# Reading the moving operand of 73 channel blocks, of the opening and of the 256-column products two rows at a time

## The chip, the cores and the metric

The kernel runs on one core of a Trainium2 chip. The time is device microseconds of one execution. The core has a matrix engine (TensorE, PE in the profile; its weight loads are listed as PEld), three engines for elementwise work (VectorE or DVE, ScalarE or ACT, GpSimd or POOL) and SyncE (SP), which issues most transfers.

## The reference

One layer of an encoder on 256 tokens of 2048 channels, in float32:

```python
proj = h @ w_in                       # 2048 x 16416: q, k, v, r, gates, hy_u, gate_logits
y_gla = _gla_branch(q, k, v, r, ...)  # gated linear attention, both directions
y_hy = _hyena_branch(hy_u, ...)       # short convolution, then two long ones by Fourier transforms
merged = g0 * (y_gla @ w_gla_o) + g1 * (y_hy @ w_hy_o)
h = _layernorm(ALPHA * h + merged @ w_out, ln1_g, ln1_b)
ff = jnp.square(jax.nn.relu(h @ w_ff1)) @ w_ff2      # 2048 -> 8192 -> 2048
h = _layernorm(ALPHA * h + ff, ln2_g, ln2_b)
```

## The kernel before

**High and low parts.** Every large product is made in three: each operand is split into a rounded part (ScalarE casts it, L104 or L1242) and what is left (VectorE subtracts, L105 or L1239), and high x high, high x low and low x high are added in PSUM. An activation such as `xT` or `hT` lies as [128, 16 k-tiles, 2 parts, 256 tokens]. In each k-tile the 256 tokens lie with the 128 even ones first and the 128 odd ones after them (for `xT`), or the first 128 and then the other 128 of the kernel's own order (for `hT`).

**Two kinds of blocks.** A weight block of 1 MB is used in one of two ways.

In a *token block* (`token_half`, L244 to L255) the activation is stationary and the weights move past it, 512 columns at a time. The weights lie in memory with even columns first, and the matmul reads them with `in_turn`: word 0 of the first row of 256, word 0 of the second, word 1 of the first, and so on. So the result has its columns in natural order. The products of the second MLP weight in the paired loop (`form_products`, L1375 to L1383) read in the same way.

In a *channel block* (`channel_products`, L187 to L200) the weights are stationary and the activation moves. For each of 16 k-tiles there is one matmul of 512 columns (the weight's high part against both parts of the activation, L193) and one of 256 (the weight's low part against the activation's high part, L197). Both read the activation straight on. The result has the token order of the activation, so `channel_sum` (L208 to L213) adds the two halves of a PSUM bank and writes q and k with every second word skipped (`in_order`, `by_parity`), which puts tokens in natural order. Channel blocks compute q and k (12 blocks, `channel_pair`) and the first MLP product f (64 blocks).

**The opening** (L336 to L342) is a product of channel kind that starts while the input still arrives: five blocks at once (the gates' low-rank part and four blocks of q), piece by piece.

**The output projection and the last product** use 256 columns of weights at a time in their last parts (`column_half`, L1072 to L1083); these weights lie in natural order and are read straight on. So are those of one 512-column part of the last product (`fourth`, L1553, which gives `token_half` the reading `lambda w: w`).

**The MLP.** `ff1_first` (L1343) makes the first 8 blocks of f. Three of them are begun with the first 128 tokens while the second 128 are still being normalised (`begin_three`, `finish_block`); the others go through `channel_products`. Then comes the paired loop `ff_pairs` (L1421) with 56 slots. A slot has 21 products of the second weight (3 + 2 groups before, 2 after) around one channel block of f. Its order is pinned by program order on all engines. In a slot VectorE splits the slot's weights (six subtractions), adds two pairs of weight units, adds f's two halves (`quad_sum`, L1247 to L1253, f's halves straight on) and, in 27 of the slots from slot 5 on, the *forms*: combinations of f that the second product needs (`forms`, L1261), which are made by VectorE, rounded by ScalarE and subtracted by VectorE again. At the ends of the seven runs of slots it also adds the seven PSUM sums of the second product into SBUF.

**Buffers around it.** Of the four PSUM buffers of the main pool three are held by the second product during the loop, so f has one: the next block of f starts when `quad_sum` has read the one before. Split weights have three buffers in turn for each part.

Of the kernel before, what the change touches and what calls it, by code (L numbers as in the profile page):

```python
# [13 lines left out]
ALU = mybir.AluOpType  # L14
DRAM = bass.MemoryType.DRAM

P = 128
D = 2048
L = 256
NT = L // P  # L20
# [11 lines left out]
LEAD = 8  # L32
# [17 lines left out]
def block_kernel(  # L50
# [128 lines left out]
        fetch()  # L179
        return queue.popleft()  # L180

    FULL = slice(0, L)

    def channel_psum(name):
        return psum_main(name).rearrange("p (a b) -> p a b", a=2)

    def channel_products(ps, act, half, kts, ts=FULL, opens=True):  # L187
        hi, lo = half
        at = [(kt, slice(kt % 8 * P, (kt % 8 + 1) * P)) for kt in kts]

        def high():
            for kt, js in at:
                MM(ps[:, :, ts], hi[:, js], act[:, kt, :, ts], start=(kt == 0 and opens), stop=(kt == KT - 1))  # L193

        def low():
            for kt, js in at:
                MM(ps[:, 0, ts], lo[:, js], act[:, kt, 0, ts], start=False, stop=False)  # L197

        for part in (high, low) if kts[0] == 0 else (low, high):
            part()  # L200

    def by_parity(ap):
        return ap.rearrange("p (t m) -> p t m", t=NT)

    def in_order(ap):
        return ap.rearrange("p (m t) -> p t m", t=NT)

    def channel_sum(dst, ps, name, scale=1.0):  # L208
        low = base.tile([P, L], F32, tag="low", name=name)
        with tc.high_priority():  # L210
            nc.scalar.activation(low, ps[:, 1], AF.Copy, scale=scale)
            nc.vector.scalar_tensor_tensor(in_order(dst), by_parity(ps[:, 0]), scale, by_parity(low),
                                           op0=ALU.mult, op1=ALU.add)  # L213

    def channel_pair(act, name, dst, scale=1.0):
        for c in range(2):
# [16 lines left out]
    def finish_block(ps, act, parts, n):  # L233
        for h in range(n):
            high_by_tokens(ps, act, parts[h], range(8 * h, 8 * h + 8), slice(P, L))
        for h in range(n):
            low_of_all(ps, act, parts[h], range(8 * h, 8 * h + 8))
        for h in range(n, 2):
            channel_products(ps, act, parts[h], range(8 * h, 8 * h + 8))

    def in_turn(w):
        return w.rearrange("p (a b) -> p b a", a=2)

    def token_half(pss, act, half, tbs, kt0, ends=(0, KT - 1), order=lambda ins: ins, moving=in_turn):  # L244
        hi, lo = half
# [54 lines left out]
    with tc.tile_pool(name="xp", bufs=1) as xp, tc.tile_pool(name="xq", bufs=1) as xq:  # L300
        def units(pool, tag, n, **kw):
            t = pool.tile([P, n, OPENING * P], F32R, tag=tag, name=f"open_{tag}", **kw)
            return lambda a, b: t[:, a:b].rearrange("p k (b j) -> p k b j", b=OPENING)

        pieces = {}
        for k0, n in PIECES[::-1]:
            if k0 < 10:
                pieces[k0] = xp.tile([P, n, KROW], F32, tag=f"xw{k0}", name=f"xw{k0}")
            else:
                raw = wp.tile([P, D], F32, tag="raw", bufs=3, name=f"xw{k0}")  # L310
                pieces[k0] = raw[:, 0:n * KROW].rearrange("p (k c) -> p k c", k=n)
        wu = xp.tile([P, 512], F32, tag="wu", name="wu")
        nc.vector.memset(wu, 0.0)
        pw = psum_side("warm")
        for _ in range(2):
            MM(pw, wu[:, 0:P], wu, start=True, stop=True)

        fetched[0] = OPENING
        for k0, n in PIECES:
            nc.sync.dma_start(pieces[k0], first[k0 * P:(k0 + n) * P, :].rearrange("(p k) c -> p k c", k=n))  # L320

        u_y, u_g, u_k, u_q, u_x = (units(base, "yT", 12), units(qp, "G", 6), units(qp, "k", 3), units(qp, "q", 2),
                                   units(xq, "sp", 3))
        places = {6: (u_y(6, 8), u_y(8, 10)), 8: (u_y(10, 12), u_g(0, 2)), 10: (u_g(2, 4), u_g(4, 6)),
                  12: (u_k(0, 2), u_q(0, 2))}
        for i in range(3):
            t = weight_half(-1, i, True)
            places[i] = [v[:, 0:OPENING * P].rearrange("p (k b j) -> p k b j", k=1, b=OPENING) for v in t]
            places[3 + i] = (u_y(2 * i, 2 * i + 1), u_y(2 * i + 1, 2 * i + 2))
        places[14], places[15] = (u_k(2, 3), u_x(0, 1)), (u_x(1, 2), u_x(2, 3))  # L330

        def part_of(kt, part):
            k0 = kt if kt in places else kt - 1
            return places[k0][part][:, kt - k0]

        def products(kts, b, part):  # L336
            for kt in kts:
                w = part_of(kt, part)[:, b]
                if part == 0:
                    MM(open_ps[b], w, xT[:, kt], start=(kt == 0), stop=(b == 0 and kt == KT - 1))  # L340
                elif b:
                    MM(open_ps[b][:, 0], w, xT[:, kt, 0], start=False, stop=(kt == KT - 1))  # L342

        turned = False
        for k0, n in PIECES:
            raw = pieces[k0]
            kts = range(k0, k0 + n)
            split_hi_lo(xT[:, k0:k0 + n, 0], xT[:, k0:k0 + n, 1], raw[:, :, 0:L])
            w = raw[:, :, L:].rearrange("p k (b j) -> p k b j", b=OPENING)

            def split(hi, lo, w, first=0):
                nc.scalar.copy(hi, w)
                if first == 0:
                    low = hi[:, :, 0, 96:]
                    nc.vector.tensor_tensor(low, w[:, :, 0, 96:], low.bitcast(F32), op=ALU.subtract)
                bs = slice(1 - first, None)
                nc.vector.tensor_tensor(lo[:, :, bs], w[:, :, bs], hi[:, :, bs].bitcast(F32), op=ALU.subtract)

            if k0 == 0:
                hi, lo = places[0]  # L360
                for bs in (slice(0, 3), slice(3, OPENING)):
                    split(hi[:, :, bs], lo[:, :, bs], w[:, :, bs], bs.start and 1)
            elif k0 == 14:
                for i in range(n):
                    split(places[k0 + i][0], places[k0 + i][1], w[:, i:i + 1])
            else:
                split(places[k0][0], places[k0][1], w)
            if k0 + n == KT:
                for b in range(OPENING):
                    for part in (0, 1):  # L370
                        products(kts, b, part)
            else:
                for part in (1, 0) if turned else (0, 1):
                    for b in range(OPENING):
                        products(kts, b, part)
                turned = not turned and k0 >= 6 and k0 < 12
# [152 lines left out]

    pa = open_ps[0]  # L530
    nc.scalar.copy(a_low, pa[:, 1])
    nc.vector.tensor_tensor(in_order(a_sum[:, 0]), by_parity(pa[:, 0]), by_parity(a_low), op=ALU.add)
    nc.scalar.copy(as_sb, a_sum[:, 0])
    nc.vector.tensor_tensor(as_sb[64:96, :], a_sum[64:96, 0], as_sb[64:96, :].bitcast(F32), op=ALU.subtract)
    pump()
# [536 lines left out]
    def column_half(pss, act, half, ch, tbs, kt0, ends=(0, KT - 1), order=lambda ins: ins):  # L1072
        hi, lo = half
        for j in range(2):
            kt = kt0 + j
            cs = slice(j * 512 + ch * 256, j * 512 + ch * 256 + 256)
            for tb in tbs:
                ps = pss[tb][ch][:, 0:256]
                sh = act[:, kt, 0, tb * P:(tb + 1) * P]
                sl = act[:, kt, 1, tb * P:(tb + 1) * P]  # L1080
                order(MM(ps, sh, hi[:, cs], start=(kt == ends[0]), stop=False))
                order(MM(ps, sh, lo[:, cs], start=False, stop=False))
                order(MM(ps, sl, hi[:, cs], start=False, stop=(kt == ends[1])))  # L1083

    def column_products(pss, act, blocks, tbs, b0):
        for ch in range(2):
# [157 lines left out]
    def rest(lo, src, hi):  # L1244
        return VT(lo, src, hi.bitcast(F32), ALU.subtract)

    def quad_sum(i, c, ps, name):  # L1247
        low = base.tile([P, L], F32, tag="low", name=name)
        dst = quads(i)[:, 2 * c:2 * c + 2][:, ::-1]
        halves = [a.rearrange("p (t j) -> p t j", j=P) for a in (ps[:, 0], low)]  # L1250
        with tc.high_priority():
            cast(low, ps[:, 1])
            return VT(dst, halves[0], halves[1], ALU.add)  # L1253
# [89 lines left out]
    def ff1_first():  # L1343
        begun = begin_three()
        for c2 in range(LEAD // 2):
            for c in range(2):
                if begun:
                    ps, parts, n = begun.pop(0)
                    finish_block(ps, hT, parts, n)
                else:  # L1350
                    ps = channel_psum(f"f{c2}_{c}")
                    parts = next_block()
                    for h in range(2):
                        channel_products(ps, hT, parts[h], range(8 * h, 8 * h + 8))
                summed = quad_sum(c2, c, ps, f"f{c2}_l{c}")
                at = 2 * c2 + c
                if at in (LEAD - 4, LEAD - 3):
                    block_load(at - LEAD + 4)
# [191 lines left out]
    add_ff(left[0], 0, 1024, 512, order=keep)  # L1550
    keep(split_hi_lo(zg[0], zg[1], z1[:, 1, 0:1024])[1])
    for half, kt in fourth:
        token_half([ps], f3, half, [0], kt, ENDS, keep, lambda w: w)  # L1553
    pss = [psum_main(f"w2_33_1{ch}") for ch in range(2)]
    add_ff(ps, 0, 1536, 512)
    rs, nb = norm_scale(st2, 0, "2")
# [54 lines left out]
def _layout(a):  # L1611
# [5 lines left out]
        k, n = w.shape  # L1617
        return w.reshape(k // P, P, n // P, P).transpose(2, 1, 0, 3).reshape(n // P, P, -1)

    def even_first(w):  # L1620
        return w.reshape(-1, 256, 2).transpose(0, 2, 1).reshape(w.shape)

    def tok(w):
        k, n = w.shape
# [14 lines left out]
    for i in range(NCH // 2):  # L1639
# [13 lines left out]
    wblk = np.concatenate(  # L1653
        [chan(ga), chan(seg["q"]), chan(seg["k"])]
        + [even_first(w) for w in [tok(seg["r"]), tok(seg["v"]), g1] + ubl + [g2, tok(a["w_hy_o"][0]), wo[:-4]]]
        + [wo[-4:], f1[:LEAD], pairs, even_first(rest[:-2]), rest[-2:]], axis=0)

    first = np.concatenate(
        [a["x"][0].T.reshape(KT, P, P, NT).transpose(1, 0, 3, 2).reshape(P, KT, L)] + [w.reshape(P, KT, P) for w in wblk[0:OPENING]], axis=2)
# [95 lines left out]
```

## Time and profile before

| | |
|---|---|
| median of 3 runs | 1726.65 us (1725.03 to 1726.79) |
| profiled execution | 1725.64 us, its span 1723.9 us |
| TensorE busy | 99% of the span, granted clock 1.00 |
| VectorE, ScalarE, GpSimd busy | 85%, 61%, 11% |
| HBM read, written | 382.12 MB, 12.06 MB |

The profile is of one execution. [...] A line that belongs to a helper (L105, L1239) collects all that goes through it; the tiles' names tell the users apart: `f` is the first MLP product, `w` the second or the last, `wo` the output projection, `wr`, `xh_r`, `xl_r`, `fraw_r` are weights of the last product that stay in SBUF, `fa` are the forms.

### The profile page before, as it was taken

Reading aid. Unit: us, or ns where it says so; the run is one execution under the profiler, and the core shown is the slowest. Engines: PE = TensorE matmul, PEld = TensorE weight load, DVE = VectorE, ACT = ScalarE, POOL = GpSimd, SP = SyncE. Lnnn points to the kernel's source line nnn. Section 1 sums busy time; section 2 is a strip of 40 time slices with the busy share of each in tenths; the row PEclk is TensorE's granted clock in tenths of the full one; section 3 lists DMA queues with packets and bytes.
Section 4 is the critical chain, followed back from the end, with each engine's and each line's share of the span. In section 5 each row is a group of like instructions: output and inputs, shape, how many; then the busy total and the mean of one; then the engine's idle time right before and its main releaser. Section 6 shows DMA issues by size and latency. Waiting matters only on the chain.

```text
span 1723.9 us, 23597 instructions
## 1 busy us (share of the span) xinstructions
PE 1712.0 (99%) x8771; PEld 1494.8 (87%) x8771; DVE 1457.2 (85%) x1899; ACT 1044.0 (61%) x1446; POOL 186.5 (11%) x243
## 2 busy tenths in 40 slices
PE   9999999999999999999999999999999999999998
PEld 7888888888888888888888889888888888888886
DVE  6788997877698989898856668889999999999998
ACT  6588886787444444444544445666766666666653
POOL 1000111000010101011000000111111112111200
PEclk9999999999999999999999999999999999999999
DMA  8677888644897969797555774687888888888864
GB/s 335 237 235 272 308 261 276 210 147 157 281 296 241 295 239 297 237 293 255 214 200 195 280 280 163 203 266 246 274 251 266 249 255 278 259 265 249 266 216 164
DMA packets 87299, 427.13 MB, mean 248 GB/s; under 512 B 9800, under 2 KB 14296, under 8 KB 45584
## 3 DMA queue, kind: packets, MB, share of 16 engines
q1 hardware_dynamic: 47664, 336.35, 52.6%
q0 software_dynamic: 30560, 67.38, 18.9%
q10 hardware_dynamic: 8960, 21.89, 3.6%
q8 instruction: 69, 1.13, 0.3%
q14 instruction: 46, 0.38, 0.1%
HBM read 382.12 MB, written 12.06 MB: 229 GB/s over the span
## 4 chain that ended last, share of the span: by engine, by line
PE 75%; DVE 6%; ACT 2%; issue 1%; DMA 1%; POOL 0%; DVEq 0%; ACTq 0%
PE f L193 12%; PE f L197 6%; PE w L1381 5%; PE w L1383 5%; PE w L1382 5%; PE ux L255 3%; PE ux L254 3%; PE ux L253 3%; PE g L254 3%; PE g L255 3%; PE g L253 3%; PE go L255 2%; PE ho L254 2%; PE go L253 2%; PE ho L253 2%; PE ho L255 2%
## 5 line engine op out<-in xcount | busy, mean ns | idle before, releaser
L104 ACT CAST whi<-raw 128x1024 fp32r<-128x1024 f32 x360 | 375.9, 1050 | 362.0 <-PE ux L255 72.6
L105 DVE TENSOR_TENSOR wlo<-raw,whi 128x1024 fp32r<-128x1024 f32 x360 | 436.6, 1219 | 134.7 <-ACT whi L104 131.8
L193 PE MATMUL f<-hT,whi 128*128 128x512 f32 x984 | 245.6, 392 | 0.1
L193 PEld LDWEIGHTS f<-hT,whi 128*128 128x128 f32 x984 | 180.0, 188 | 35.7 <-DVE sum_fr L1239 1.1
L1239 DVE TENSOR_TENSOR wlo<-fraw,whi 128x1024 fp32r<-128x1024 f32 x112 | 136.6, 1220 | 11.1 <-ACT whi L1242 7.8
L1242 ACT CAST whi<-ring 128x1024 fp32r<-128x1024 f32 x56 | 58.9, 1052 | 122.7 <-DVE ring L1239 122.7
L197 PEld LDWEIGHTS f<-hT,wlo 128*128 128x128 f32 x984 | 123.8, 188 | 5.2
L1302 POOL DMA_DIRECT2D ring<-wblk x56 | 48.6, 868 | 708.1 <-DVE ring L1239 460.7
L197 PE MATMUL f<-hT,wlo 128*128 128x256 f32 x984 | 124.9, 279 | 0.0
L1242 ACT CAST whi<-fraw 128x1024 fp32r<-128x1024 f32 x112 | 117.5, 1049 | 0.2 <-PE w L1383 0.2
L254 PE MATMUL g<-wlo,xT 128*128 128x512 f32 x256 | 97.6, 381 | 0.8 <-DVE wlo L105 0.8
L1242 ACT CAST b_h<-ring 128x1024 fp32r<-128x1024 f32 x112 | 87.8, 833 | 16.3 <-PE w L1383 9.4
L255 PE MATMUL ux<-whi,xT 128*128 128x512 f32 x256 | 97.3, 380 | 0.0
L254 PE MATMUL ux<-wlo,xT 128*128 128x512 f32 x256 | 97.3, 380 | 0.0
L255 PE MATMUL g<-whi,xT 128*128 128x512 f32 x256 | 97.1, 379 | 0.0
L253 PE MATMUL g<-whi,xT 128*128 128x512 f32 x256 | 89.5, 380 | 0.0
L253 PE MATMUL ux<-whi,xT 128*128 128x512 f32 x256 | 86.6, 379 | 0.0
L1239 DVE TENSOR_TENSOR ring<-ring 128x512 f32<-128x512 f32 x112 | 77.0, 687 | 1.9
L1239 DVE TENSOR_TENSOR b_l<-ring,b_h 128x1024 fp32r<-128x1024 f32 x56 | 68.2, 1219 | 5.1 <-ACT b_h L1242 5.1
L1239 DVE TENSOR_TENSOR wlo<-ring,whi 128x1024 fp32r<-128x1024 f32 x56 | 68.6, 1224 | 2.2 <-ACT whi L1242 0.3
L1239 DVE TENSOR_TENSOR fa<-ring,fa 128x1024 fp32r<-128x1024 f32 x56 | 68.2, 1218 | 0.0
L1303 POOL DMA_DIRECT2D ring<-ring x56 | 67.2, 1201 | 0.0
(529 smaller groups left out, 4227.0 us busy)
## 6 DMA issues: line engine op xcount, KB each, us to landing
raw<-wblk SPq DMA_DIRECT2D x188, 1024.0 KB, 5.3
fraw<-wblk SPq DMA_DIRECT2D x56, 1024.0 KB, 4.9
ring<-wblk SPq DMA_DIRECT2D x56, 1024.0 KB, 7.2
ring<-wblk POOLq DMA_DIRECT2D x56, 256.0 KB, 4.6
ring<-ring POOLq DMA_DIRECT2D x56, 256.0 KB, 5.3
conv_sb<-conv_rows SPq DMA_DIRECT2D x12, 1024.0 KB, 8.7
w<-w4s ACTq DMA_DIRECT2D x16, 512.0 KB, 5.6
Td<-T POOLq DMA_DIRECT2D x32, 256.0 KB, 5.1
```

The costliest lines, as they stand in the source:

```text
L104: return (nc.scalar.copy(hi, src), nc.vector.tensor_tensor(lo, src, hi.bitcast(F32), op=ALU.subtract))
L105: nc.vector.tensor_tensor(lo, src, hi.bitcast(F32), op=ALU.subtract))
L193: MM(ps[:, :, ts], hi[:, js], act[:, kt, :, ts], start=(kt == 0 and opens), stop=(kt == KT - 1))
L197: MM(ps[:, 0, ts], lo[:, js], act[:, kt, 0, ts], start=False, stop=False)
L253: order(MM(pss[tb], sh, wh, start=(kt == ends[0]), stop=False))
L254: order(MM(pss[tb], sh, wl, start=False, stop=False))
L255: order(MM(pss[tb], sl, wh, start=False, stop=(kt == ends[1])))
L1239: return pin(nc.vector.tensor_tensor(dst, a, b, op=op))
L1242: return pin(nc.scalar.copy(hi, src))
L1381: pin(MM(ps, sh, wh, start=(p == begin), stop=False))
L1382: MM(ps, sh, wl, start=False, stop=False)
L1383: pin(MM(ps, sl, wh, start=False, stop=(p == end - 1)))
```

## The change

The rows of 128 tokens of an activation (at a distance of 128 words) are now read in turn, word by word, by the 512- and 256-column matmuls of the channel blocks and of the opening; so are the two rows of 128 columns of the 256-column products, whose weights lie in memory with even columns first within each 256. The results of the channel blocks then have tokens in the other order. For q, k and the gates this is the natural one, and their sums read and write straight on. For f the sum now reads every second word of PSUM and of its partner in SBUF, to write f in the order that it had. The three blocks that are begun early stay as they were (`plain`). Every engine executes the same instructions in the same order with the same waits as before; only the addresses they step through differ.

```diff
-    def channel_products(ps, act, half, kts, ts=FULL, opens=True):
+    def in_turn(w):
+        return w.rearrange("p (a b) -> p b a", a=2)
+
+    def both_in_turn(t):
+        return t.rearrange("p k (a b) -> p k b a", a=2)
+
+    def channel_products(ps, act, half, kts, plain=False):
...
-                MM(ps[:, :, ts], hi[:, js], act[:, kt, :, ts], start=(kt == 0 and opens), stop=(kt == KT - 1))
+                MM(ps, hi[:, js], act[:, kt] if plain else both_in_turn(act[:, kt]), start=(kt == 0), stop=(kt == KT - 1))
...
-                MM(ps[:, 0, ts], lo[:, js], act[:, kt, 0, ts], start=False, stop=False)
+                MM(ps[:, 0], lo[:, js], act[:, kt, 0] if plain else in_turn(act[:, kt, 0]), start=False, stop=False)
...
-            nc.vector.scalar_tensor_tensor(in_order(dst), by_parity(ps[:, 0]), scale, by_parity(low),
-                                           op0=ALU.mult, op1=ALU.add)
+            nc.vector.scalar_tensor_tensor(dst, ps[:, 0], scale, low, op0=ALU.mult, op1=ALU.add)
...
-            channel_products(ps, act, parts[h], range(8 * h, 8 * h + 8))
+            channel_products(ps, act, parts[h], range(8 * h, 8 * h + 8), plain=True)
...
-                    MM(open_ps[b], w, xT[:, kt], start=(kt == 0), stop=(b == 0 and kt == KT - 1))
+                    MM(open_ps[b], w, both_in_turn(xT[:, kt]), start=(kt == 0), stop=(b == 0 and kt == KT - 1))
...
-                    MM(open_ps[b][:, 0], w, xT[:, kt, 0], start=False, stop=(kt == KT - 1))
+                    MM(open_ps[b][:, 0], w, in_turn(xT[:, kt, 0]), start=False, stop=(kt == KT - 1))
...
-    nc.vector.tensor_tensor(in_order(a_sum[:, 0]), by_parity(pa[:, 0]), by_parity(a_low), op=ALU.add)
+    nc.vector.tensor_tensor(a_sum[:, 0], pa[:, 0], a_low, op=ALU.add)
...
-                order(MM(ps, sh, hi[:, cs], start=(kt == ends[0]), stop=False))
-                order(MM(ps, sh, lo[:, cs], start=False, stop=False))
-                order(MM(ps, sl, hi[:, cs], start=False, stop=(kt == ends[1])))
+                wh, wl = in_turn(hi[:, cs]), in_turn(lo[:, cs])
+                order(MM(ps, sh, wh, start=(kt == ends[0]), stop=False))
+                order(MM(ps, sh, wl, start=False, stop=False))
+                order(MM(ps, sl, wh, start=False, stop=(kt == ends[1])))
...
-        halves = [a.rearrange("p (t j) -> p t j", j=P) for a in (ps[:, 0], low)]
+        halves = [a.rearrange("p (t j) -> p t j" if plain else "p (j t) -> p t j", j=P) for a in (ps[:, 0], low)]
...
-        token_half([ps], f3, half, [0], kt, ENDS, keep, lambda w: w)
+        token_half([ps], f3, half, [0], kt, ENDS, keep, lambda w: both_in_turn(w.rearrange("p (k c) -> p k c", k=2)))
...
-        + [wo[-4:], f1[:LEAD], pairs, even_first(rest[:-2]), rest[-2:]], axis=0)
+        + [even_first(wo[-4:], 256), f1[:LEAD], pairs, even_first(rest[:-2]), even_first(rest[-2:], 256)], axis=0)
```

More of the change, by code (lines that the diff above doesn't have):

```diff
@@ L180, in next_block @@
         return queue.popleft()
-    FULL = slice(0, L)
     def channel_psum(name):
         return psum_main(name).rearrange("p (a b) -> p a b", a=2)
-    def channel_products(ps, act, half, kts, ts=FULL, opens=True):
+    def in_turn(w):
[3 more added lines that the diff above has]
+    def channel_products(ps, act, half, kts, plain=False):
         hi, lo = half
@@ L192, in high @@
             for kt, js in at:
-                MM(ps[:, :, ts], hi[:, js], act[:, kt, :, ts], start=(kt == 0 and opens), stop=(kt == KT - 1))
+                MM(ps, hi[:, js], act[:, kt] if plain else both_in_turn(act[:, kt]), start=(kt == 0), stop=(kt == KT - 1))
         def low():
             for kt, js in at:
-                MM(ps[:, 0, ts], lo[:, js], act[:, kt, 0, ts], start=False, stop=False)
+                MM(ps[:, 0], lo[:, js], act[:, kt, 0] if plain else in_turn(act[:, kt, 0]), start=False, stop=False)
         for part in (high, low) if kts[0] == 0 else (low, high):
             part()
[L202 to L206, printed above, removed]
     def channel_sum(dst, ps, name, scale=1.0):
@@ L238, in finish_block @@
         for h in range(n, 2):
-            channel_products(ps, act, parts[h], range(8 * h, 8 * h + 8))
-    def in_turn(w):
-        return w.rearrange("p (a b) -> p b a", a=2)
+            channel_products(ps, act, parts[h], range(8 * h, 8 * h + 8), plain=True)
     def token_half(pss, act, half, tbs, kt0, ends=(0, KT - 1), order=lambda ins: ins, moving=in_turn):
@@ L1245, in rest, with quad_sum @@
         return VT(lo, src, hi.bitcast(F32), ALU.subtract)
-    def quad_sum(i, c, ps, name):
+    def quad_sum(i, c, ps, name, plain=False):
         low = base.tile([P, L], F32, tag="low", name=name)
         dst = quads(i)[:, 2 * c:2 * c + 2][:, ::-1]
-        halves = [a.rearrange("p (t j) -> p t j", j=P) for a in (ps[:, 0], low)]
+        halves = [a.rearrange("p (t j) -> p t j" if plain else "p (j t) -> p t j", j=P) for a in (ps[:, 0], low)]
         with tc.high_priority():
@@ L1346, in ff1_first @@
             for c in range(2):
+                plain = bool(begun)
                 if begun:
@@ L1354, in ff1_first @@
                         channel_products(ps, hT, parts[h], range(8 * h, 8 * h + 8))
-                summed = quad_sum(c2, c, ps, f"f{c2}_l{c}")
+                summed = quad_sum(c2, c, ps, f"f{c2}_l{c}", plain)
                 at = 2 * c2 + c
@@ L1618, in chan, with even_first @@
         return w.reshape(k // P, P, n // P, P).transpose(2, 1, 0, 3).reshape(n // P, P, -1)
-    def even_first(w):
-        return w.reshape(-1, 256, 2).transpose(0, 2, 1).reshape(w.shape)
+    def even_first(w, n=512):
+        return w.reshape(-1, n // 2, 2).transpose(0, 2, 1).reshape(w.shape)
     def tok(w):
```

## The prediction

> **What bounds the kernel now.** I read the page's busy times first, then the table by stretches (length, then busy time of PE, PEld, DVE, ACT and POOL), the timeline of TensorE, and the waits of VectorE.
>
> ```profile
> PE 1712.0 (99%) x8771; PEld 1494.8 (87%) x8771; DVE 1457.2 (85%) x1899; ACT 1044.0 (61%) x1446; POOL 186.5 (11%) x243
> 33.00:104.00 71.00, 71.00 (x409) 61.82 (x408) 51.96 (x77) 47.07 (x75) 4.58 (x9) 1.00 0.69 243
> 1055.00:1103.00 48.00, 48.00 (x325) 44.26 (x324) 39.77 (x65) 30.82 (x49) 1.79 (x2) 1.00 0.54 181
> 1103.00:1153.00 50.00, 50.00 (x265) 43.80 (x264) 44.18 (x54) 35.99 (x48) 8.74 (x10) 1.00 0.79 243
> 1153.00:1667.00 514.00, 513.62 (x2700) 449.26 (x2699) 483.79 (x616) 345.71 (x461) 87.87 (x100) 1.00 0.83 257
> ```
>
> PE is busy in 1712.0 of 1723.9 us. In the stretch where q and k are computed (33 to 104) and in the whole first MLP product (1055 to 1667) it has next to no gaps, so a matmul that gets shorter there shortens the kernel, as long as something else does not take its place. The candidate is VectorE (DVE): 44.18 of 50 us in the first slots of the paired loop, and 483.79 of 514 us in the rest of it. A busy PE is not a fast PE, so next comes the distance between the starts of successive matmuls. First one slot of the paired loop, then the place near the end where the two ways of reading stand side by side on the same lines.
>
> ```profile
> 1292.37 0.38 PE L1381 MATMUL w<-fa 128*128 128x512 f32 x1
> ...
> 1296.69 0.38 PE L1383 MATMUL w<-whi,fa 128*128 128x512 f32 x1
> 1296.90 2.00 PE L193 MATMUL f<-hT,whi 128*128 128x512 f32 x8
> 1298.74 2.03 PE L197 MATMUL f<-hT,wlo 128*128 128x256 f32 x16
> 1300.60 2.00 PE L193 MATMUL f<-hT,whi 128*128 128x512 f32 x8
> 1302.44 0.38 PE L1381 MATMUL w<-fa 128*128 128x512 f32 x1
> ```
> ```profile
> 1700.26 0.40 PE L255 MATMUL w<-wr,fa 128*128 128x512 f32 x1
> ...
> 1702.32 0.39 PE L255 MATMUL w<-wr,fa 128*128 128x512 f32 x1
> 1702.54 0.38 PE L253 MATMUL w<-xh_r,fa 128*128 128x512 f32 x1
> ...
> 1707.51 0.38 PE L255 MATMUL w<-fa,fa 128*128 128x512 f32 x1
> ```
>
> The columns are start, length, engine, line, tiles. In the slot, 21 products of 512 columns that read two rows of 256 in turn (L1381 to L1383) take 1296.90 - 1292.37 = 4.53 us, 215.7 ns each. The 16 products of L193 read 512 columns straight on and take 1.84 us for 8, 230 ns each. The 16 of L197, 256 columns straight on, take 1.86 us, 116.3 ns each. That this is the reading and not the kind of block, the second fence shows: `wr` is read straight on, 9 distances in 2.06 us, 229 ns; `xh_r` and the tiles after it are read in turn by the same lines with the same stationary tile, 23 distances in 4.97 us, 216 ns. Straight reading costs 14.3 ns in 512 columns here, in turn costs none of it.
>
> **The change part by part.** No instruction is added, removed or moved on any engine. What changes is the order of reading, in three places, and the order in which some sums are read and written.
>
> ```profile
> L193 PE MATMUL f<-hT,whi 128*128 128x512 f32 x984 | 245.6, 392 | 0.1
> L193 PE MATMUL k<-xT,whi 128*128 128x512 f32 x128 | 31.0, 391 | 0.0
> L193 PE MATMUL q<-xT,whi 128*128 128x512 f32 x64 | 15.9, 393 | 0.0
> ```
>
> *One channel block.* It is 16 products of 512 and 16 of 256 columns. If two rows of 128 read in turn behave as two rows of 256 do, the first fall from 230 to 215.7 ns: 16 x 14.3 = 0.229 us. For 256 columns in turn the trace has no row. The bounds are 116.3 ns (nothing gained) and half of 215.7, 107.9 ns; a loss in proportion to the columns gives 7.15 ns off, 109.2 ns, and I take that, as it goes by the row of the same kernel with the same cause: 16 x 7.15 = 0.114 us. A block gains 0.343 us. By the counts there are 984/16 = 61.5 blocks of f (one half of one stays plain, so 61: 5 before the paired loop, 56 in it), 8 of k and 4 of q.
>
> *Is 128 like 256?* That is the assumption of the whole sum. For it: both patterns alternate between two places word by word, and both read each word once. [...]
>
> *q and k* (33 to 104 us, PE without a gap, DVE 51.96 of 71): 12 blocks x 0.343 = 4.1 us. Their sums (L212) now read and write straight on; they read straight and wrote every second word before, and take as long as the sums of f, whose rows were straight on both sides, so nothing is gained there:
>
> ```profile
> L212 DVE SCALAR_TENSOR_TENSOR k_sb<-k,k_l 128x256 f32<-128x256 f32 x8 | 3.4, 422 | 3.3 <-ACT k_l L211 3.3
> L1239 DVE TENSOR_TENSOR dftl_fr<-f,f_l 128x256 f32<-128x256 f32 x26 | 10.9, 419 | 4.7 <-ACT f_l L1242 4.7
> ```
>
> *The opening.* 80 products of 512 and 64 of 256, at the same two distances:
>
> ```profile
> 12.31 1.32 PE L340 MATMUL open<-xT,open_yT 128*128 128x512 f32 x5
> 13.47 0.64 PE L342 MATMUL open<-xT,open_yT 128*128 128x256 f32 x4
> 13.95 1.32 PE L340 MATMUL open<-xT,open_yT 128*128 128x512 f32 x5
> ```
>
> Five and four take 1.64 us together, 5 x 230 + 4 x 117, with no wait in between. 80 x 14.3 + 64 x 7.15 = 1.6 us. If the pieces of the input turn out to set the pace, it is 0.
>
> *256-column products* of the output projection (L1081 to L1083, 192 of them) and of the last product (48):
>
> ```profile
> 1038.11 0.28 PE L1081 MATMUL wo<-wr,mT 128*128 128x256 f32 x1
> ...
> 1039.55 0.28 PE L1081 MATMUL wo<-wr,mT 128*128 128x256 f32 x1
> ```
>
> Twelve distances in 1.44 us, 120 ns each. With 7.15 ns off: 192 x 7.15 = 1.4 us and 48 x 7.15 = 0.3 us. The 12 products of 512 columns on `wr` gain nothing, since the next tile of `wr` is waited for anyway.
>
> *Before the paired loop* 5 blocks: 1.7 us. *The first five slots* hold no forms of the second weight, and DVE has room: 5 x 0.343 = 1.7 us.
>
> *The other 51 slots.* PE would save 51 x 0.343 = 17.5 us. Here DVE is late next. A slot waits for DVE's sum of f, since f has one PSUM buffer: the channel products of the next slot start only when the sum has read it.
>
> ```profile
> 1305.37 0.41 DVE L1239 TENSOR_TENSOR dftl_fr<-f,f_l 128x256 f32<-128x256 f32 x1
> PEld f L193 <- DVE sum_fr L1239: 1.1, 3, 0.5
> DVE fa L1239 <- ACT fa L1242: 10.8, 26, 0.6
> DVE wlo L1239 <- ACT whi L1242: 6.6, 15, 0.5
> DVE b_l L1239 <- ACT b_h L1242: 2.8, 5, 0.8
> DVE dfth_fr L1239 <- ACT f_l L1242: 1.1, 5, 0.2
> DVE dftl_fr L1239 <- ACT f_l L1242: 0.9, 4, 0.2
> ```
>
> In the slot shown, the last of f's matmuls was issued before 1302.44, yet the sum starts at 1305.37: DVE is behind by 2.9 us, and three times in the program PE already waited for such a sum (1.1 us). The waits of DVE from 1153 to 1667 are the last five rows. The first, 10.8 us, stays whatever PE does: DVE writes, ScalarE rounds, DVE goes on. The other four, 6.6 + 2.8 + 1.1 + 0.9 = 11.4 us, fall where DVE has caught up and the tile or the sum to be read comes from PE's progress. So DVE can give at most 11.4 us, 0.22 per slot. From this goes what its own sums grow: they now read every second word, from PSUM and from SBUF. Rows for a VectorE and a ScalarE read of every second word, beside straight ones of the same size:
>
> ```profile
> L105 DVE TENSOR_TENSOR stl<-st,sth 128x512 fp32r<-128x512 f32 x4 | 3.2, 809 | 4.0 <-ACT sth L104 3.9
> L105 DVE TENSOR_TENSOR xT<-xw,xT 128x512 fp32r<-128x512 f32 x5 | 3.4, 685 | 1.0 <-ACT xT L104 1.0
> L104 ACT CAST sth<-st 128x512 fp32r<-128x512 f32 x4 | 3.6, 894 | 0.6 <-DVE st L688 0.6
> L104 ACT CAST xT<-xw 128x512 fp32r<-128x512 f32 x5 | 3.1, 621 | 2.8 <-DMA xw<-first 2.8
> ```
>
> 809 against 685 ns for 512 columns is +62 ns for 256; 894 against 621 is a factor of 1.44, +0.18 us on 0.41. The lower end is 0 (a gain is excluded, since the row before was straight). I take 62 ns, the row of the same engine: 51 x 0.062 = 3.2 us. DVE can then give 11.4 - 3.2 = 8.2 us of the 17.5. Forms come in runs of two and three slots, in which DVE falls behind, and not every wait between them can be used: I take 7.
>
> Sum: 1.6 + 4.1 + 1.4 + 1.7 + 1.7 + 7 + 0.3 = 17.8 us. The profiled execution took 1725.6, so 1707.8; the median of the runs, 1726.65, is 1.0 above it, and the forecast is 1709.
>
> **The rivals.**
>
> *DVE does not hold it.* If the casts can run ahead and the sums cost nothing more, the 51 slots give all 17.5 us instead of 7, and the time is 1698. For it speaks that DVE is busy 94% and not 100%; against it the sum at 1305.37 and the waits of PE.
>
> *Rows of 128 words apart gain nothing.* Then PE stays as it is, the sums' 62 ns per slot fit into DVE's 0.22 us, and the time is 1726 to 1728. Nothing in the trace reads at that distance, so nothing excludes it.
>
> *The sums get dear: slower.* Place: DVE in the 51 slots. What the other parts give is 17.8 - 7 = 10.8 us; DVE's room is 0.22 us per slot. The change is a loss from a price of 0.22 + 10.8/51 = 0.43 us more per sum, twice its present 0.41. If a sum took three times as long (+0.82), the 51 slots lose 51 x (0.82 - 0.22) = 31 us and the time is 1726.65 + 31 - 10.8 = 1747. Against it are the two rows above, which stay under a factor of 1.5. They are reads of SBUF; no row reads every second word of PSUM. [...]
>
> *In turn at 128 words collides: slower.* If TensorE paid what ScalarE pays for every second word, the factor 1.44, a block would grow from 5.54 to 8.0 us, 73 blocks by 2.4 us, 178 us in all: 1904. [...]
>
> **How the numbers follow.** The forecast has 0.70, DVE not holding it 0.13, no gain 0.09, dear sums 0.05, a collision 0.03. The smallest gain within the forecast: 256 columns gain nothing (a block 0.229 us), sums at +0.18. Opening 1.1, q and k 2.7, the five blocks 1.1, the first slots 1.1, the others 11.4 - 51 x 0.18 = 2.2: 8.2 us, 1718.4. The largest is the second case, 1698. The range 1698 to 1719 holds these two cases, 0.83. Within 0.2%, 3.5 us, which is about what a measurement of this kernel can tell from no change, lies the third case, 0.09; slower are the last two, 0.08; faster 0.83.
>
> **What would show it.** Right: distances of about 216 ns on the lines of the channel products and the opening, near 109 on those of 256 columns; a slot of about 9.9 us; DVE above 97% from slot 6 on, its waits for ScalarE's casts of weights mostly gone, and more waits of PE for the sum of f. The sums of f near 0.48 us, those of q and k unchanged. Wrong: distances of 230 ns as before (the assumption on 128 words fails); a slot of 9.73 us with PE still without gaps (the second case); sums of f near 0.8 us or more.

## The result, and the profile after

| | before | after |
|---|---|---|
| median (lowest to highest of 4 runs) | 1726.27 us (1725.03 to 1726.79) | 1715.31 us (1714.65 to 1715.51) |
| profiled execution, its span | 1725.64, 1723.9 us | 1715.43, 1713.6 us |

After is 0.9937 of before, 95% interval 0.992 to 0.9954: 11.0 us faster, in the range, 6 us short of the forecast. All times here and below are of fast runs; one run of `before_squares`, 3605.11 us, was slow and is left out. The medians of the kernel before lie at 1726.3, 1725.9 and 1726.9 us beside the different groups of runs, so times of different groups compare to about 1 us.

First the rate of the matmuls. The timeline of TensorE after (start, length, engine, line, operation, tiles, shape, count, and in brackets the wait ahead of it), in slot 20, the one behind the slot shown of before (slots are numbered from 0):

```profile
1295.67 1.99 PE L197 MATMUL f<-hT,whi 128*128 128x512 f32 x8
1297.50 1.95 PE L201 MATMUL f<-hT,wlo 128*128 128x256 f32 x16
1299.29 1.89 PE L197 MATMUL f<-hT,whi 128*128 128x512 f32 x8
1301.02 0.38 PE L1377 MATMUL w<-fa 128*128 128x512 f32 x1
...
1306.50 1.99 PE L197 MATMUL f<-hT,whi 128*128 128x512 f32 x8 [0.79 <-DVE sum_fr L1234]
1308.34 1.95 PE L201 MATMUL f<-hT,wlo 128*128 128x256 f32 x16
```

Eight products of 512 columns take 1301.02 - 1299.29 = 1.73 us, 216 ns each (230 before). Sixteen of 256 take 1299.29 - 1297.50 = 1.79, 112 ns (over all 61 blocks 111.5, and 116.6 before). The block is 0.30 us shorter. But the slot from 1295.67 ends only at 1306.50: 10.83 us, where before it was 10.07, because TensorE now waits 0.79 us for VectorE's sum of f. Where no such wait stands a slot takes 9.77 us.

The table of stretches says the same of the fifty slots 5 to 54. The columns are the stretch, its length, busy time of PE, PEld, DVE, ACT and POOL with their counts, granted clock, DMA share and GB/s; before, then after:

```profile
1155.49:1660.50 505.01, 504.62 (x2651) 441.37 (x2650) 474.82 (x606) 340.59 (x454) 87.87 (x100) 1.00 0.84 258
```
```profile
1146.16:1649.55 503.39, 494.63 (x2651) 436.69 (x2649) 476.75 (x605) 338.65 (x453) 87.83 (x100) 1.00 0.84 259
```

TensorE was busy in all but 0.4 us of these slots; now 8.8 us are gaps, and the slots together are 1.6 us shorter, not 50 x 0.30 = 15. The 50 slots stand 14.9 us above 50 x 9.77 (more than the gaps, since the matmul ahead of one is listed 0.38 us long where the next could start after 0.22, and the first half of f behind one takes 1306.50 to 1308.34, 1.84 us, instead of 1.73). The waits that end the gaps, by the view of waits for these slots of after (who waits, for whom, total, times, longest):

```profile
DVE fa L1234 <- ACT fa L1237: 10.8, 26, 0.6
PEld f L197 <- DVE dftl_fr L1234: 7.3, 12, 1.1
PEld f L197 <- DVE sum_fr L1234: 4.8, 4, 1.2
DVE wlo L1234 <- ACT whi L1237: 4.6, 10, 0.5
PE f L197 <- DVE sum_fr L1234: 3.2, 4, 0.8
PE f L197 <- DVE dftl_fr L1234: 2.8, 4, 0.7
DVE b_l L1234 <- ACT b_h L1237: 1.7, 2, 1.0
```

`dftl_fr`, `dfth_fr` and `sum_fr` are the tiles into which f's sums are written. These sums are a little longer, as this group of VectorE's instructions after shows (418 ns before; the fifty of the loop take 471 on average):

```profile
L1234 DVE TENSOR_TENSOR dfth_fr<-f,f_l 128x256 f32<-128x256 f32 x26 | 12.2, 470 | 1.5 <-ACT f_l L1237 1.4
```

Where the time came from, by the first matmul of each stage in the two timelines (the gains are taken from unrounded times):

| stretch | before | after | gained | forecast |
|---|---|---|---|---|
| start to q (opening) | 31.8 | 31.0 | 0.8 | 1.6 |
| q to r (the q, k blocks) | 72.6 | 68.9 | 3.6 | 4.1 |
| r to the output projection | 863.5 | 863.1 | 0.4 | 0 |
| output projection to f | 87.7 | 86.1 | 1.6 | 1.4 |
| f to slot 0 (five blocks) | 50.7 | 49.4 | 1.3 | 1.7 |
| slots 0 to 4 | 49.2 | 47.6 | 1.6 | 1.7 |
| slots 5 to 54 | 505.0 | 503.4 | 1.6 | 7 (51 slots) |
| slot 55 to the end | 63.4 | 64.0 | -0.6 | 0.3 |

Outside slots 5 to 54, all but the opening and the end came within 0.5 us of the forecast. At the end the 256-column products do get shorter, from 120 to 111 ns, but behind them TensorE waits 0.96 us for VectorE's `fin` where before it waited 0.41. The main question is why the fifty slots gave 1.6 us.

### The profile page after: what moved, and what is told of

It is laid out like the page before. It is cut to its first block, busy times and chain, and to the rows that moved or that the text cites. A ratio compares the mean times of both kernels' runs of the same rounds, so it can differ in the third digit from the quotient of the medians.

```text
span 1713.6 us, 23597 instructions
## 1 busy us (share of the span) xinstructions
PE 1691.5 (99%) x8771; PEld 1486.1 (87%) x8771; DVE 1459.7 (85%) x1899; ACT 1041.8 (61%) x1446; POOL 186.5 (11%) x243
## 4 chain that ended last, share of the span: by engine, by line
PE 55%; DVE 18%; ACT 6%; issue 4%; DMA 1%; POOL 0%; ACTq 0%; DVEq 0%
PE f L197 6%; ACT whi L1237 4%; PE ux L249 3%; PE ux L247 3%; PE ux L248 3%; PE g L248 3%; DVE wlo L1234 3%; PE g L249 3%; PE g L247 3%; PE f L201 3%; DVE fa L1234 2%; DVE ring L1234 2%; DVE b_l L1234 2%; PE go L247 2%; PE ho L249 2%
## 5 line engine op out<-in xcount | busy, mean ns | idle before, releaser
L197 PE MATMUL f<-hT,whi 128*128 128x512 f32 x984 | 234.0, 381 | 6.9 <-DVE sum_fr L1234 3.2
L201 PEld LDWEIGHTS f<-hT,wlo 128*128 128x128 f32 x984 | 119.5, 192 | 3.3
L201 PE MATMUL f<-hT,wlo 128*128 128x256 f32 x984 | 119.9, 275 | 0.0
L1237 ACT CAST b_h<-ring 128x1024 fp32r<-128x1024 f32 x112 | 87.7, 832 | 10.7 <-PE w L1379 5.4
```

What stands on the lines that cost most here:

```text
L197: MM(ps, hi[:, js], act[:, kt] if plain else both_in_turn(act[:, kt]), start=(kt == 0), stop=(kt == KT - 1))
L201: MM(ps[:, 0], lo[:, js], act[:, kt, 0] if plain else in_turn(act[:, kt, 0]), start=False, stop=False)
L1237: return pin(nc.scalar.copy(hi, src))
```

## The experiments

Three explanations were put against each other. One: an order problem. VectorE and ScalarE wait for one another within a slot, and what ScalarE has queued ahead of its copy of f's lower half makes the sum late; TensorE's slack of 0.3 us per slot had hidden that. Two: VectorE has too much work for a slot of 9.77 us. Three: the sums, now 50 ns longer, use up the gain.

**The change without its part in f** (`rest_only`): f's blocks read straight on again, all else as after.

```diff
-                plain = bool(begun)
+                plain = True
...
-                channel_products(ps, hT, half_parts.pop((s, h)), range(8 * h, 8 * h + 8))
+                channel_products(ps, hT, half_parts.pop((s, h)), range(8 * h, 8 * h + 8), plain=True)
...
-            quad_sum(n, c, ps, f"f{n}_l{c}")
+            quad_sum(n, c, ps, f"f{n}_l{c}", True)
```

> The changed kernel with f's channel blocks straight on again (their sums too); opening, q, k and the 256-column products stay in turn. If the parts add up as the two traces show them (f's first product starts 6.4 us earlier than before: opening 0.8, q and k 3.7, the rest columns and drift), this run gains 6 to 7 us over before (ratio 0.996) and the paired loop has its old slot of 10.07 us. The rival, that f's blocks bring most of the 11 us and the other parts little, would give 2 to 4 us.

Measured: 1719.21 us, ratio to before 0.9962 (0.995 to 0.9975), 6.7 us faster than the 1725.91 us of before beside it, which is the 6 to 7 us expected from the parts. The slots are back at 10.07 us, and slots 5 to 54 take 504.7 us. So the reading of f, in 61 blocks that are 0.30 us shorter each, is worth 1719.21 - 1715.31 = 3.9 us of a possible 61 x 0.30 = 18.3.

**The sums' reading given back** (`sum_write`): f's sum reads straight on, and writes the two rows of its tile in turn.

```diff
-        halves = [a.rearrange("p (t j) -> p t j" if plain else "p (j t) -> p t j", j=P) for a in (ps[:, 0], low)]
+        halves = [a.rearrange("p (t j) -> p t j" if plain else "p (j t) -> p j t", j=P) for a in (ps[:, 0], low)]
+        if not plain:
+            dst = dst.rearrange("p t j -> p j t")
```

> The changed kernel, but f's sum reads straight on and puts the tokens in order as it writes (every second word goes to the other row). Theory 1: in the paired loop the chain of VectorE and ScalarE work is the bound, a period of ten slots takes 100.7 us because that is what this chain takes; then 52 ns less per sum over 51 slots is 2.6 us less: 1712.7. Theory 2: VectorE has room, TensorE waits only because the sum comes late in slots with forms and f has one PSUM buffer; then only the 25 or so slots with that wait gain, 1.3 us: 1714. If writing out of order costs what reading out of order does, nothing changes: 1715.3.

Measured: 1718.47 us, ratio 0.9952 (0.994 to 0.9965), later than every expectation. The sums did not get cheaper but dearer; a group of them, and the table of stretches for the same fifty slots, of this kernel:

```profile
L1234 DVE TENSOR_TENSOR dftl_fr<-f,f_l 128x256 f32<-128x256 f32 x26 | 15.9, 610 | 3.5 <-ACT f_l L1237 3.5
```
```profile
1150.18:1654.48 504.30, 495.09 (x2652) 436.65 (x2650) 481.80 (x606) 339.22 (x454) 87.83 (x100) 1.00 0.84 258
```

A sum takes 619 ns in the loop, 148 more than after. That is 50 x 0.148 = 7 us more work, and VectorE's busy time is 5.1 us longer (481.80 against 476.75). Yet the fifty slots are only 0.9 us longer. This speaks against three, and against two as well: 5 us of work more on an engine that sets the pace would show as 5 us. With one it agrees: in ten of the slots VectorE waits for ScalarE's next cast right behind the sum, and there the longer sum only shortens that wait (`wlo` for `whi`, 4.6 us after and 3.2 here). Of the 3.2 us between the medians most is not in the slots. In the profiled execution of `sum_write` the stretch from v to the scores (`s`), from 206 to 309 us, is 3.9 us longer than after, and TensorE's granted clock from 200 to 311 is 0.98 there and 1.00 after. The same shows in `sum_first` (5.5 us, 0.97) and in `sum_between` (3.7 us, 0.98); in the other profiles here the clock is 1.00. The stretch lies far from the edits. So from here on the fifty slots are compared beside the times.

**The squares early** (`squares_early`): ScalarE squares a finished block of f ahead of the casts of the next pair's weights, not behind them.

```diff
+            if c == 0 and s:
+                squares(n - 1)
             if more:
                 pair_split(s + 1)
             take_sums(pss, s, (3, 4))
-            if c == 0 and s:
-                squares(n - 1)
```

> The changed kernel, with the two ScalarE steps that square f's sums put ahead of the cast of the pair weights, where ScalarE waits 2 us for VectorE anyway. In the trace of the changed kernel nine slots with squares and no forms have VectorE waiting 0.23 us for ScalarE's copy of f's low half and 0.46 us for the weight cast after it. Theory 1 (the chain is the bound): these 9 x 0.69 = 6.2 us come off, 1709. Theory 2 (the late sum and the one buffer are the bound, which is met in slots with forms): no change within 1 us, 1715.

Measured: 1706.96 us, ratio 0.9889 (0.9874 to 0.9904), faster than the changed kernel by 8.4 us, more than the 6.2 that the first theory gave. The trace shows how. Slot 18 after, ScalarE, then VectorE; its block of f starts at 1275.80:

```profile
1281.34 1.05 ACT L1237 CAST whi<-ring 128x1024 fp32r<-128x1024 f32 x1 [2.19 <-PE f L197]
1282.30 0.62 ACT L1252 ACTIVATE dfth_fr<-dfth_fr 128x512 f32<-128x512 f32 x1
1282.95 0.64 ACT L1253 ACTIVATE dfth_fr<-dfth_fr 128x512 f32<-128x512 f32 x1
1283.49 0.36 ACT L1237 COPY f_l<-f 128x256 f32<-128x256 f32 x1
1283.74 1.05 ACT L1237 CAST whi<-fraw 128x1024 fp32r<-128x1024 f32 x1
```
```profile
1279.84 1.41 DVE L1234 TENSOR_TENSOR ring<-ring 128x512 f32<-128x512 f32 x2
...
1283.88 0.49 DVE L1234 TENSOR_TENSOR dftl_fr<-f,f_l 128x256 f32<-128x256 f32 x1 [0.23 <-ACT f_l L1237]
1284.82 1.23 DVE L1234 TENSOR_TENSOR wlo<-fraw,whi 128x1024 fp32r<-128x1024 f32 x1 [0.46 <-ACT whi L1237]
```

ScalarE stands idle for 2.19 us and only then does the cast and the two squares, though what they square has long been there. The row names a product of f as what ended this wait, but the cast reads `ring`, and VectorE's additions into `ring` end at 1279.84 + 1.41 = 1281.25, 0.09 us ahead of the cast. In all fifty slots, before and after, the cast starts 0.09 us behind these additions, and the view of waits of before names them in all fifty (113.6 us in total, the longest 4.0):

```profile
ACT whi L1242 <- DVE ring L1239: 113.6, 50, 4.0
```

So ScalarE waits for VectorE here, not for TensorE. The copy `f_l` and the next cast stand behind the squares; VectorE waits for the first 0.23 us and for the second 0.46. TensorE had issued the last product of this block before 1281.15, 2.3 us ahead of the copy. The same slot with the squares early, where the block of f starts at 1274.53, ScalarE and VectorE:

```profile
1277.22 0.63 ACT L1252 ACTIVATE dfth_fr<-dfth_fr 128x512 f32<-128x512 f32 x1
1279.50 1.04 ACT L1237 CAST whi<-ring 128x1024 fp32r<-128x1024 f32 x1 [0.99 <-DVE ring L1234]
1280.45 0.36 ACT L1237 COPY f_l<-f 128x256 f32<-128x256 f32 x1
```
```profile
1278.01 1.41 DVE L1234 TENSOR_TENSOR ring<-ring 128x512 f32<-128x512 f32 x2
...
1281.72 0.49 DVE L1234 TENSOR_TENSOR dftl_fr<-f,f_l 128x256 f32<-128x256 f32 x1
```

The cast again starts 0.08 us behind the additions (1278.01 + 1.41 = 1279.42), this time while f's products still run. The squares fill the idle time, the sum starts 7.19 us behind the start of the block instead of 8.08, and VectorE waits for neither the copy nor the next cast. It starts the next slot's work that much earlier, and what it has then is what the slots with forms use up. Over the fifty slots VectorE's wait for `whi` falls from 4.6 to 0.8 us and TensorE's gaps from 8.8 to 3.5. The slots take 494.6 us, 8.8 less than after.

**The same edit on the kernel before** (`before_squares`), to see whether it is a gain of its own.

> The kernel before, with one edit: ScalarE does the squares of a gate block ahead of the casts of the next pair's weights, not behind them. Theory (a chain VectorE - ScalarE - VectorE that only shows once TensorE is faster): before the change TensorE sets the loop, its slots take 10.07 us and 50 of them 503.5 of the 505.0 us that slots 5 to 55 take, so at most 1.5 us can be won: 1724.4 to 1726. Rival (the squares are a gain by themselves, whatever TensorE reads): the 8.4 us they were worth after the change, 1717.6.

Measured: 1725.8 us (ten runs), ratio 0.9992 (0.9983 to 1.0001), as the theory has it. The fifty slots of this kernel:

```profile
1157.79:1661.71 503.92, 503.92 (x2652) 441.83 (x2651) 475.98 (x608) 344.19 (x455) 88.02 (x100) 1.00 0.85 259
```

1.1 us less than before, and TensorE without any gap: the slots were bound by it, and the order on ScalarE cost nothing until TensorE got faster.

**The sum ahead of the forms** (`sum_first`): in slots with forms VectorE and ScalarE do f's sum before any part of the forms.

```diff
+            quad_sum(n, c, ps, f"f{n}_l{c}")
             if s in FORMED:
                 forms(FORMED[s])
-            quad_sum(n, c, ps, f"f{n}_l{c}")
```

> The changed kernel, with f's sum ahead of the forms in the slots that have both, on VectorE and on ScalarE. The work of VectorE stays the same. Theory 1 (the chain is the bound): the wait for the sum goes, and as much comes back at other tiles that VectorE delivers; the loop stays within 1.5 us, 1714 to 1717. Theory 2 (order and the one buffer): the sum is read 2.5 us earlier, the waits of TensorE before f's products go, and the loop's slots come to 9.77 us; up to 14.9 us of waits are in the loop, VectorE's idle time allows some 8: 1707.

Measured: 1721.27 us, ratio 0.9974 (0.9965 to 0.9983), slower than the changed kernel by 6 us; the fifty slots take 508.6, 5.2 more. Neither expectation held. The longest of these waits in the fifty slots, of TensorE and of VectorE:

```profile
PEld w L1378 <- DVE wlo L1234: 11.5, 20, 0.9
DVE wlo L1234 <- ACT whi L1237: 10.2, 37, 0.5
```

TensorE no longer waits for the sum but for the split weights `wlo`, which VectorE makes behind the forms, and VectorE waits for ScalarE's casts of weights more than after (10.2 us against 4.6). That is the mechanism of the first theory, with a larger bill: an earlier sum is worth nothing if it makes the next thing late by as much or more.

**The sum within the forms** (`sum_between`): the squares early, and the sum placed where VectorE has finished the three small subtractions of the forms and waits for ScalarE to round them.

```diff
-    def forms(n):
+    def forms(n, between=lambda: None):
...
         VT(t[:, 2], q[:, 3], q[:, 0], ALU.subtract)
+        between()
         for part, c in ((q, slice(0, 4)), (t, slice(4, 7))):
...
-                forms(FORMED[s])
-            quad_sum(n, c, ps, f"f{n}_l{c}")
+                forms(FORMED[s], lambda: quad_sum(n, c, ps, f"f{n}_l{c}"))
+            else:
+                quad_sum(n, c, ps, f"f{n}_l{c}")
```

> The changed kernel with the squares early and one more edit: in slots with forms the sum of f (ScalarE's copy and VectorE's addition) stands between the three subtractions of the forms and the casts of the forms, where VectorE waits 0.41 us for ScalarE. With the squares early alone, slots 5 to 55 take 494.6 us, 6.0 over what TensorE needs (50 x 9.77 = 488.6), all of it in the second and third slots of a run of forms. Theory (VectorE and ScalarE wait for each other there): the sum fills these waits and ends some 1.65 us earlier, so 4 to 6 us go: 1701 to 1703. Rival (VectorE is short of time, not badly ordered; the forms, now 0.5 us later, are waited for instead): 1707 or above.

Measured: 1703.13 us, ratio 0.986 (0.9846 to 0.9873), at the upper end of the theory's 1701 to 1703 and the fastest of the kernels that compute everything. VectorE in slot 20, with the sum between the forms' small operations and their roundings, which it no longer waits for:

```profile
1303.84 0.29 DVE L1234 TENSOR_TENSOR dftl_fr<-dftl_fr,fw 128x128 f32<-128x128 f32 x1
1304.38 0.48 DVE L1234 TENSOR_TENSOR sum_fr<-f,f_l 128x256 f32<-128x256 f32 x1
1304.88 0.69 DVE L1234 TENSOR_TENSOR fa<-dftl_fr,fa 128x512 fp32r<-128x512 f32 x1
```

The fifty slots, and all of VectorE's waits in them:

```profile
1150.48:1639.11 488.63, 488.63 (x2651) 439.01 (x2650) 476.37 (x607) 344.02 (x455) 88.03 (x100) 1.00 0.87 267
```
```profile
DVE wlo L1234 <- ACT whi L1237: 5.5, 26, 0.4
DVE b_l L1234 <- ACT b_h L1237: 1.3, 3, 0.6
```

Every slot takes 9.77 us, and TensorE has no gap. VectorE does the same work as after, 476.4 us against 476.8, now in 488.6 us instead of 503.4. That decides against explanation two: VectorE had the time, in another order.

**Without most forms** (`few_forms`): to see the floor from the other side, the forms are left out. The edit keeps those of slots 5, 6, 8 and 9 and leaves out the other 23, so it starts at slot 10 and not at 14, as the text below has it.

```diff
-            if s in FORMED:
+            if FORMED.get(s, 8) < 8:
```

> The changed kernel without the forms of the second weight from slot 14 on (their place in SBUF keeps what the first ones wrote, so the output is not the reference's): VectorE loses 5 operations, 2.2 us, and one wait in 19 slots. Theory (what keeps the slots above 9.77 us is VectorE and ScalarE, and the forms are what makes them late): every slot from 14 on takes 9.77 us; they stand 13.4 us above it now, so 1702. Rival (TensorE itself is held by what it reads, since sums and products use the same rows): the slots keep their length, 1715.

Measured: 1701.76 us, ratio 0.9855 (0.984 to 0.987). Every slot from 11 on takes 9.77 us, as in `sum_between`: leaving the forms out wins no more than ordering them well. The slots did not keep their length, so TensorE is not held by what it reads.

**Other orders of reading** (`patterns`, `patterns2`): distances between matmuls only. The edit of the second, number of rows and words in each for 512 and for 256 columns; the first has other orders in the same places.

```diff
+    WAYS = {"q": ((2, 64), (2, 64)), "k": ((4, 128), (2, 32)), "f": ((2, 8), (2, 2))}
...
+                        MM(ps, hi[:, js], rows_turned(act[:, kt].rearrange("p k t -> p (k t)"), *two), start=(kt == 0), stop=(kt == KT - 1))
...
+                        MM(ps[:, 0], lo[:, js], rows_turned(act[:, kt, 0], *one), start=False, stop=False)
```

> A look at distances between matmuls, not at the time. The changed kernel, in which q's blocks read four rows of 64 words in turn, k's 512-column products eight rows of 32 in turn and its 256-column products two words of each of two rows in turn, and the 5 blocks of f ahead of the paired loop every second word of a row, then the others; the columns of q, k and these f come out in another order than the reference's. Straight reading is 230 ns for 512 columns and 116 for 256; two rows in turn 216 and 111. If any change of place between words does it: 216 and 111 everywhere. If it takes two places at least 128 words apart: 230 and 116 for every second word (2 words apart) and for short rows. If neighbouring words are what costs: 216 for every second word and for rows in turn, 114 for two words of each row.

> Again a look at distances alone. In the run before, four rows of 64 words in turn took 283 and 143 ns for 512 and 256 columns, eight rows of 32 took 437, every second word 451 and 229, two words of each of two rows 174 for 256: all slower than straight on. Here the number of places and their distance are taken apart. q: two rows of 64 words in turn, then the next two, for both widths. k: four rows of 128 in turn for 512 columns, two rows of 32 for 256. f ahead of the paired loop: two rows of 8 words in turn for 512, two rows of 2 words for 256. If the number of places decides: 216 and 111 for two rows at any distance, 283 for four rows of 128. If the distance decides: four rows of 128 take 216, two rows of 64 take 283 and 143, and it grows as the rows get shorter. The columns of q, k and these f come out in another order than the reference's.

TensorE's timeline of the first (L209 is 512 columns, L211 is 256; q is four rows of 64 in turn, then k and f):

```profile
35.55 4.70 PE L209 MATMUL q<-xT,whi 128*128 128x512 f32 x16
40.08 2.46 PE L211 MATMUL q<-xT,wlo 128*128 128x256 f32 x16
42.37 4.70 PE L209 MATMUL q<-xT,whi 128*128 128x512 f32 x16
...
58.90 3.68 PE L209 MATMUL k<-xT,whi 128*128 128x512 f32 x8
62.39 2.96 PE L211 MATMUL k<-xT,wlo 128*128 128x256 f32 x16
65.17 7.21 PE L209 MATMUL k<-xT,whi 128*128 128x512 f32 x16
...
1120.85 7.40 PE L209 MATMUL f<-hT,whi 128*128 128x512 f32 x16
1128.07 3.84 PE L211 MATMUL f<-hT,wlo 128*128 128x256 f32 x16
1131.73 3.79 PE L209 MATMUL f<-hT,whi 128*128 128x512 f32 x8
```

And of the second (L204 is 512 columns, L206 is 256):

```profile
34.63 3.62 PE L204 MATMUL q<-xT,whi 128*128 128x512 f32 x16
38.09 1.95 PE L206 MATMUL q<-xT,wlo 128*128 128x256 f32 x16
39.88 3.62 PE L204 MATMUL q<-xT,whi 128*128 128x512 f32 x16
...
54.97 1.95 PE L206 MATMUL k<-xT,wlo 128*128 128x256 f32 x16
56.76 4.68 PE L204 MATMUL k<-xT,whi 128*128 128x512 f32 x16
61.28 0.50 PE L206 MATMUL k<-xT,wlo 128*128 128x256 f32 x3
...
1082.95 3.62 PE L204 MATMUL f<-hT,whi 128*128 128x512 f32 x16
1086.40 2.03 PE L206 MATMUL f<-hT,wlo 128*128 128x256 f32 x16
1088.27 3.62 PE L204 MATMUL f<-hT,whi 128*128 128x512 f32 x16
```

Each distance is the difference of two starts over the count, for instance (40.08 - 35.55) / 16 = 283 ns:

| order of words | 512 columns | 256 columns |
|---|---|---|
| straight on | 230 ns | 116 ns |
| two rows in turn, 128 or 256 words apart | 216 | 111 to 112 |
| two rows in turn, 64 words apart | 216 | 112 |
| two rows in turn, 32 words apart | | 112 |
| two rows in turn, 8 words apart | 216 | |
| two rows in turn, 2 words apart | | 117 |
| two words of each of two rows in turn | | 174 |
| four rows in turn, 64 words apart | 283 | 143 |
| four rows in turn, 128 words apart | 282 | |
| eight rows in turn, 32 words apart | 436 | |
| every second word | 451 | 229 |

None of the three expectations of the first run held: every order tried there is slower than straight on. The second run bears out the number of places: of rows read one word each in turn, their number decides here and not their distance (two rows 216 ns at 8 to 256 words, four rows 283 and 282 at 64 and 128), with one exception, two rows 2 words apart, which are read like straight ones (117 ns for 256 columns). Two words of each row and every second word are slower than straight on, and this rule does not cover them.

## Why the prediction was right, and where it was wrong

**Right: two rows of 128 are read as two rows of 256 are.** 216 ns, as assumed, and the two rows can be as near as 8 words (216 ns for 512 columns in `patterns2`). Two rows in turn, 8 words apart or more, are the fastest order tried, while every second word costs nearly double the straight reading (451 against 230 ns).

**Mis-sized: the 256-column products.** 7.15 ns off was taken by proportion to the columns; in the channel blocks it is 5.1 (116.6 to 111.5), in the range of the two bounds given. A block gains 0.30 us and not 0.343, which is 0.5 us in q and k, 0.2 in the five blocks and 2 us in what the slots could have had. In the output projection it is 9 (120 to 111), and 1.6 us came for a forecast of 1.4.

**The opening.** 0.8 us instead of 1.6. The text held 0 for the case that the input sets the pace, and in this execution a wait of 0.63 us for ScalarE's cast of a piece stands at 9.18 us. It differs from one execution to the next: in the eight other profiles with this opening q starts at 30.3 to 31.1 us, 0.6 to 1.5 ahead of the 31.8 of before.

**Right: the sums.** +53 ns (471 against 418 in the loop) for a forecast of +62. The rival of dear sums needed 430 ns more. The 53 ns are for a sum that reads both PSUM and SBUF out of order, and no run here takes the two apart.

**Wrong: "The other four, 6.6 + 2.8 + 1.1 + 0.9 = 11.4 us, fall where DVE has caught up and the tile or the sum to be read comes from PE's progress."** From this came "DVE can give at most 11.4 us", and the 7 us taken of it; the slots gave 1.6. In the fifty slots these four waits were 6.1 + 2.8 + 1.1 + 0.9 = 10.9 us before, and they still are 4.6 + 1.7 + 1.1 + 0.9 = 8.3 us after. In all, VectorE's idle time there fell by 3.6 us (505.01 - 474.82 = 30.2 before, 503.39 - 476.75 = 26.6 after); 1.9 of it became busy time, with sums that are 50 x 0.053 = 2.7 us longer, and 1.6 shorter slots. The rows named ScalarE as the one waited for, and that was the literal truth: the copy and the cast behind it are late because ScalarE has other work, the squares, ahead of them and behind a wait of 2.19 us for VectorE's own additions. A shorter block on TensorE does not shorten such a wait of VectorE and ScalarE for each other. With nothing but the squares moved, the fifty slots fall by 8.8 us in the changed kernel, and by 1.1 in the kernel before.

**Wrong as well: "The first, 10.8 us, stays whatever PE does."** It did stay (10.8 after), but as a property of the order and not of the work: with the sum placed into it, it is gone, and the fifty slots go from 494.6 to 488.6 us. "At most 11.4" was no upper bound for VectorE, whose idle time in the fifty slots was 30.2 us before.

**Luck in the total.** The time lies in the range although the largest term, 7 us of 17.8, gave 1.6. The lower end of the range had 2.2 us for these slots, but from sums that grow by 0.18 us each; they grew by 0.05, and the slots stayed long for another reason.

**The rival "DVE does not hold it"** had 17.5 us in the slots for its condition that casts can run ahead. With the order repaired the fifty slots give 505.0 - 488.6 = 16.4 us, so its size was about right (1.5 us of it are waits that stood there before the change, 505.0 - 50 x 10.07) and its condition needed two edits that were not part of this change.

**The signs named for it.** Distances, sums of f and more waits of TensorE for them came about as written. "A slot of about 9.9 us" did not: the mean is 503.39 / 50 = 10.07. Nor did "DVE above 97%" (476.75 of 503.39 us is 94.7%) and "its waits for ScalarE's casts of weights mostly gone" (`wlo` 6.1 us before, 4.6 after). The share came with `sum_between` (476.37 of 488.63, 97.5%); those waits went with `squares_early` (0.8 us) and are back in `sum_between` (5.5 us), where they cost nothing. They were to be the signs of a VectorE at its limit, and it was not.

Not settled: why two places are read faster than one and four slower, why TensorE's granted clock was lower between 200 and 311 us in three of the profiles, and what else lengthens that stretch (in `before_squares` v to the scores is 1.5 us longer than before, at a clock of 1.00).

## What to carry to other kernels

Before a faster TensorE is counted on, walk one slot of the engine next in line and ask of each of its waits what the engine waited for has queued ahead: a wait that has room to hide today becomes the bound tomorrow, and it falls by moving work in the queue, not by a faster producer. Busy time below the slot's length shows that an engine could keep up; whether it does is a matter of order (VectorE's 476 to 477 us of work took the fifty slots 503.4 us after, and 488.6 in `sum_between`), and work that is ready should stand in front of a wait, not behind it. And moving an operation earlier helps only into idle time: the sum in front of the forms lost 5.2 us in the fifty slots against the changed kernel, the same sum in the middle of them won 6.0 on top of the squares. The two were tried on different kernels, with the squares late and early, and not the other way round.

## What the runs showed of the hardware

- Of the orders tried, TensorE reads fp32r from SBUF fastest with two places in turn: 216 ns for 512 columns at 8, 64, 128 and 256 words apart, 111 to 112 for 256 columns at 32, 64 and 128; at 2 words apart 256 columns take 117. Straight on costs 230 and 116 to 120, four places in turn 283 and 143, eight 436, every second word 451 and 229.
- In the channel blocks the cost of straight reading is not in proportion to the columns: 14 ns in 512, 5 in 256. In the 256-column products of the output projection it is 9.
- VectorE adding 256 columns of PSUM and SBUF: 418 ns straight on, 471 reading every second word of both, 619 reading straight and writing two rows in turn (means of the fifty in the loop).
